# Opening the first dense unit ahead, a norm row earlier on ScalarE, transposes in another bank, and first loads from two queues

## The chip, the cores and the metric

The kernel runs on one core of a Trainium2 chip. A core has five engines that run side by side and meet through semaphores: TensorE (PE, matrix products into PSUM banks; its weight loads are listed apart as PEld), VectorE (DVE), ScalarE (ACT), GpSimd (POOL) and SyncE (SP). DMAs are issued here from SP's, ACT's and POOL's instruction streams. The metric is the time of one execution on the device, in microseconds; lower is better.

## The reference

One block of a streaming encoder, float32, 1024 frames of 1024 channels, 256 memory tokens. Cut to what matters here:

```python
h = _rmsnorm(x, norm_mix_g)
z = h @ w_in                          # 1024 x (7 * 512 + 8 + 512 + 3 * 1024)
(hq, hf, hi, hg, fq, fk, fv, ff, mq, gate_logits) = split(z)
y_a = _hgrn2_mixer(hq, hf, hi, hg, lower_bounds, hgrn_norm_g)
y_b = _fox_mixer(fq, fk, fv, ff, fox_f_bias, fox_q_norm_g, fox_k_norm_g)
mem_kv = _rmsnorm(mem, norm_mem_g) @ mem_kv_w
y_c = _memory_mixer(mq, mem_kv, mem_q_norm_g, mem_k_norm_g)
gates = sigmoid(gate_logits)
merged = gates[0] * (y_a @ w_br_hgrn) + gates[1] * (y_b @ w_br_fox) + gates[2] * (y_c @ w_br_mem)
x = x + merged @ w_out
x = x + _conv_glu_ffn(_rmsnorm(x, norm_ffn_g), w_up, conv_w, conv_b, w_down)
```

## The kernel before

Channels lie on the 128 partitions, time runs along a row. x comes as eight chunks `xk[k]` of 128 channels by 1024 frames. The norm's gain is multiplied in at once (`uh`, `ul`), and the factor 1/rms per frame is applied later, to the products. Every float32 product is made of three: an operand is split into a rounded high part and the rest, as `uh`/`ul` for x and `wh`/`wl` for weights, and `mm3` (lines 160 to 162) issues high by high, low by high and high by low. A split is a cast on ScalarE (line 166) and a subtraction on VectorE (line 174).

The part around the change is the first 100 us, up to the second dense unit:

1. The first loads: the constants `cv` (the gains among them), the first weights `wg` and the x chunks, in the order in which they are wanted. Twelve dull products (line 265) go ahead on TensorE.
2. Gate steps `s0` to `s7`: two gate chunks at once, step k with x chunk k, in four PSUM banks (two "lg", one "tr", one "po"). A step is 12 products; step k needs `uh[k]` and `ul[k]`, made by `x_chunk` (lines 346 and 347) in halves for k = 0 and 1.
3. The memory's keys and values: eight chunks `wkv` of weights (`kv_chunk`).
4. The cover: two gate chunks (`first_cover`, `gates_early`), whose products run while the x norm's factor is made. The norm: eight rows of squares (`x_square`), `rt` = (mean + eps) to the power -1/2 on POOL (line 179), then `spread_dma`: TensorE transposes `rt` (352), ScalarE copies the transpose into a row (353), two DMAs take it through DRAM into `rx`, on all partitions. Each finished gate product is then multiplied by `rx` on VectorE (461) and goes through tanh on ScalarE (462); until that has read its bank, the bank is taken.
5. The keys' transposes, in two groups of four (`mem_keys`, 410), each read out by ScalarE into `mkf` (412).
6. Dense units: a unit computes 256 channels by 1024 frames as a 2x2 product of blocks with seven products instead of eight, named by their right operand: B11, T1, T2, B22, T3, B21, T4. The T's are differences of blocks of x (`differences`, made once, in steps f1 to f3 and a last one); the left operands are the four weight blocks a11, a21, a22, a12 and their sums s1 = a21 + a22, s2 = s1 + a11, s4 = s2 + a12, s3 = a11 + a21, each split. Some products accumulate on others' banks; `snap` copies a bank ("fe") before. B21 needs nothing but a12 and x, and stands second in the first unit, sixth in the others.

What sets the order: the code issues steps in the order of the string SEQ. A planner with its own model of time then orders the instructions within each engine's stream, under the constraints of the data and of `issue_after` (an instruction that must not be placed before a given one). PSUM banks of a tag rotate.

Of the kernel before, what the change touches and what calls it, by code (L numbers as in the profile page):

```python
# [8 lines left out]
F32 = mybir.dt.float32  # L9
# [5 lines left out]
P = 128  # L15
# [76 lines left out]
def run_all(gen):  # L92
    for _ in gen:
        pass
# [15 lines left out]
def tile_block(ctx: ExitStack, tc: tile.TileContext, xT, memT, x_rows, mem_rows, vec, fbias, mats, hmask, w_first, w_cm, w_hi, w_fqk, w_fv,  # L110
# [20 lines left out]
    def ps_tr():  # L131
        return pz.tile([P, HB], F32, tag="tr", name="tr", bufs=2)
# [217 lines left out]
    def spread_dma(r, rcol, row, name, ps):  # L350

        PE.transpose(ps[:8, :P], rcol, ident)
        S.copy(row, ps[:8, :P])
# [50 lines left out]
    def mem_keys():  # L404
        mkt = keys[0]
        for hh in range(2):
            ptr = ps_tr()
            for h in range(2):
                for m in range(2):
                    PE.transpose(ptr[:, (2 * h + m) * P:(2 * h + m + 1) * P],  # L410
                                 mkt[:, m, (2 * hh + h) * P:(2 * hh + h + 1) * P], ident)
            S.activation(mkf[:, 2 * hh:2 * hh + 2, :], ptr.rearrange("p (h m) -> p h m", h=2), AF.Copy, scale=mgk)
        G.dma_start(kvd[:, 0, :], mkf.rearrange("p a b -> p (a b)"))
# [87 lines left out]
    def family_block(name, k, src, sub=None):  # L501
        h, l = fam[name]
        return split(S, h[k], l[k], src, sub)

    def differences():
# [21 lines left out]
        for k, (t2, b12, b21, b22) in enumerate(b):  # L527
            with tc.issue_after(late["x mean"].ins):
                V.scalar_tensor_tensor(out=b12, in0=b12, scalar=ngx[:, k:k + 1], in1=b22, op0=ALU.mult, op1=ALU.add)
            family_block("T3", k, b12)  # L530
        yield
        yield
        for k, (t2, b12, b21, b22) in enumerate(b):
# [5 lines left out]
            family_block("T4", k, t4[k])  # L539
        yield  # L540

    gen = {}

    def families_step():
        if "differences" not in gen:
            gen["differences"] = differences()
        next(gen["differences"])

    named = dict(f1=families_step, f2=families_step, f3=families_step, mn=mem_norm, me=keys_out, mk=mem_keys, mv=mem_values, xn=x_norm, lk=load_late, lx=lambda: load_rows(*T2[2:], *T1[2:]), ly=lambda: load_rows(*T2[:2]), lz=lambda: load_rows(*T2[2:]), ev=first_gates, cv=first_cover)
    for what in SEQ:  # L550
        if what in named:
            named[what]()
        else:
            steps[what[0]](int(what[1]))
    p0.release()

    ps1 = Rounded(tc, name="ps1", bufs=1, side="right", reuse_waits="tile")
    def block(b, k):
        if b in fam:
            return [t[k] for t in fam[b]]  # L560
# [10 lines left out]
    class Dense:  # L571
# [1 line left out]
        half = None  # L573

        def snap(self, ps):
            e = ps1.tile([P, HB], F32, tag="fe", name="fe", bufs=3)
# [6 lines left out]
        def sum_of(self, i, a, b):  # L583
            t = ps1.tile([P, HB], F32, tag=f"s{i}", name=f"s{i}")
            V.tensor_add(t, a, b)
            return t

        def operand(self, src):
# [6 lines left out]
            split(S, h, l, src)  # L595
            return h, l

    dense = Dense()

    def dense_unit(src, put, first, families):  # L600

        raw = []
        whole = None if first else dense.raw()
        for i in range(2):
            if first:
                t = wp.tile([P, 4 * 264], F32, tag="raw", name="raw", bufs=2)[:, :2 * HB]
                t = t.rearrange("p (a b) -> p a b", a=2)
            else:
                t = whole[:, 2 * i:2 * i + 2, :]
            G.dma_start(t, src[:, 2 * i:2 * i + 2, :])  # L610
            raw += [t[:, 0, :], t[:, 1, :]]
        a11, a21, a22, a12 = raw
        x, y = ps_proj(), ps_lg()
        o1 = dense.operand(a11)
        if first:
            o6 = dense.operand(a12)
        s1 = dense.sum_of(1, a21, a22)
        o2 = dense.operand(s1)
        s2 = dense.sum_of(2, s1, a11)
# [1181 lines left out]
```

## Time and profile before

| | |
|---|---|
| time, median of 3 runs | 1702.75 us (1702.54 to 1703.31) |
| the profiled execution's own time | 1703.12 us |
| its span, first to last instruction | 1701.3 us |
| TensorE busy | 1692.3 us, 99% |
| VectorE, ScalarE, GpSimd busy | 1151.9, 801.5, 326.7 us |
| granted TensorE clock | 1.00 throughout |

In rows of the profile, the first number is a start in us, the second a duration, then come engine, line of the kernel, operation, output and inputs, their shapes, and a count; what stands in square brackets is how long the engine had been idle before and what it had waited for. A product's duration is longer than its distance from the next one, as products overlap.

### The profile page before, as it was taken

Reading aid. Unit: us, or ns where it says so; the run is one execution under the profiler, and the core shown is the slowest. Engines: PE = TensorE matmul, PEld = TensorE weight load, DVE = VectorE, ACT = ScalarE, POOL = GpSimd, SP = SyncE. Lnnn points to the kernel's source line nnn. Section 1 sums busy time; section 2 is a strip of 40 time slices with the busy share of each in tenths; the row PEclk is TensorE's granted clock in tenths of the full one; section 3 lists DMA queues with packets and bytes.
Section 4 is the critical chain, followed back from the end, with each engine's and each line's share of the span. In section 5 each row is a group of like instructions: output and inputs, shape, how many; then the busy total and the mean of one; then the engine's idle time right before and its main releaser. Section 6 shows DMA issues by size and latency. Waiting matters only on the chain.

```text
span 1701.3 us, 24306 instructions
## 1 busy us (share of the span) xinstructions
PE 1692.3 (99%) x8965; PEld 1452.3 (85%) x8965; DVE 1151.9 (68%) x2057; ACT 801.5 (47%) x1428; POOL 326.7 (19%) x420
## 2 busy tenths in 40 slices
PE   9999999999999999999999999999999999999999
PEld 7788899989898998888888888888888888888887
DVE  6956555665666655786856855987778888775664
ACT  6734455555464553776531334644434444433432
POOL 0200022543433331553310000311111111100000
PEclk9999999999999999999999999999999999999999
DMA  9433242221312111200346552566555444494782
GB/s 369 170 137 114 73 146 76 77 92 45 99 50 87 52 57 57 67 27 18 100 125 216 165 188 99 162 171 172 151 144 141 118 144 147 162 375 142 247 274 87
DMA packets 82774, 227.16 MB, mean 134 GB/s; under 512 B 9680, under 2 KB 12248, under 8 KB 82528
## 3 DMA queue, kind: packets, MB, share of 16 engines
q1 hardware_dynamic: 64464, 160.99, 27.4%
q0 software_dynamic: 18048, 64.50, 13.5%
q8 instruction: 70, 1.15, 0.3%
q14 instruction: 48, 0.39, 0.1%
q10 hardware_dynamic: 144, 0.13, 0.0%
HBM read 180.72 MB, written 67.93 MB: 146 GB/s over the span
## 4 chain that ended last, share of the span: by engine, by line
PE 98%; DVE 1%; DMA 0%; ACT 0%; issue 0%; SPq 0%; DVEq 0%
PE pp L162 21%; PE pp L160 21%; PE pp L161 21%; PE lg L160 4%; PE lg L162 4%; PE lg L161 4%; PE tr L160 3%; PE tr L162 3%; PE tr L161 3%; PE po L951 1%; PE lg L910 1%; PE lg L909 1%; PE po L950 1%; PE po L160 1%; PE po L161 1%; PE po L162 1%
## 5 line engine op out<-in xcount | busy, mean ns | idle before, releaser
L160 PE MATMUL pp<-uh,wh 128*128 128x512 f32 x412 | 163.1, 396 | 0.0
L161 PE MATMUL pp<-ul,wh 128*128 128x512 f32 x412 | 162.9, 395 | 0.0
L162 PE MATMUL pp<-uh,wl 128*128 128x512 f32 x412 | 162.4, 394 | 0.0
L161 PE MATMUL pp<-wl,uh 128*128 128x256 f32 (+1 forms) x512 | 146.2, 286 | 0.0
L162 PE MATMUL pp<-wh,ul 128*128 128x256 f32 (+1 forms) x512 | 146.0, 286 | 0.0
L160 PE MATMUL pp<-wh,uh 128*128 128x256 f32 (+1 forms) x512 | 145.6, 285 | 0.0
L166 ACT CAST wh<-s 128x512 fp32r<-128x512 f32 x113 | 68.2, 620 | 130.8 <-PE pp L161 66.4
L166 ACT CAST wh<-raw 128x1024 fp32r<-128x1024 f32 (+2 forms) x76 | 67.7, 890 | 100.3 <-PE pp L161 88.2
L166 ACT CAST wh<-rw 128x512 fp32r<-128x512 f32 x87 | 53.2, 619 | 107.6 <-PE pp L161 72.0
L160 PEld LDWEIGHTS pp<-wh,uh 128*128 128x128 f32 x512 | 97.3, 190 | 1.2
L161 PEld LDWEIGHTS pp<-wl,uh 128*128 128x128 f32 x512 | 97.4, 190 | 1.0
L162 PEld LDWEIGHTS pp<-wh,ul 128*128 128x128 f32 x512 | 97.4, 190 | 0.9
L1443 POOL DMA_DIRECT2D rw<-in_w_up x44 | 24.1, 555 | 372.8 <-DVE wl L1336 171.8
L166 ACT CAST dwh<-wr 128x1024 fp32r<-128x1024 f32 (+1 forms) x41 | 40.2, 980 | 115.0 <-PE tr L161 40.4
L162 PEld LDWEIGHTS pp<-uh,wl 128*128 128x128 f32 x412 | 77.5, 188 | 15.1
L174 DVE TENSOR_TENSOR wl<-raw,wh 128x1024 fp32r<-128x1024 f32 (+2 forms) x75 | 78.0, 1040 | 18.1 <-ACT wh L166 17.9
L160 PEld LDWEIGHTS pp<-uh,wh 128*128 128x128 f32 x412 | 77.5, 188 | 14.6
L161 PEld LDWEIGHTS pp<-ul,wh 128*128 128x128 f32 x412 | 77.5, 188 | 14.5
L174 DVE TENSOR_TENSOR dwl<-wr,dwh 128x1024 fp32r<-128x1024 f32 (+1 forms) x41 | 46.3, 1130 | 33.6 <-ACT dwh L166 32.5
L925 ACT ACTIVATE pt<-pt,st 128x128 f32<-128x128 f32 (+3 forms) x64 | 49.7, 777 | 40.1 <-DVE st L922 32.0
L927 POOL TENSOR_SCALAR pt<-pt,st 128x128 f32<-128x128 f32 (+3 forms) x64 | 50.7, 793 | 77.5 <-DVE st L926 62.4
L1336 DVE TENSOR_TENSOR wl<-rw,wh 128x512 fp32r<-128x512 f32 x69 | 47.7, 705 | 22.5 <-PE pp L162 18.1
(497 smaller groups left out, 5123.9 us busy)
## 6 DMA issues: line engine op xcount, KB each, us to landing
rw<-in_w_up POOLq DMA_DIRECT2D x44, 512.0 KB, 4.9
sd<-in_w_dn POOLq DMA_DIRECT2D x30, 512.0 KB, 6.2
br<-yd SPq DMA_DIRECT2D x30, 512.0 KB, 5.3
raw<-in_w_cm SPq DMA_DIRECT2D x24, 512.0 KB, 3.4
gd<-gt SPq DMA_DIRECT2D x48, 256.0 KB, 2.0
gt<-gd SPq DMA_DIRECT2D x48, 256.0 KB, 2.7
yd<-fc SPq DMA_DIRECT2D x44, 256.0 KB, 3.0
wr<-sd SPq DMA_DIRECT2D x20, 512.0 KB, 4.6
```

The lines of the kernel that those rows point to most:

```text
L160: PE.matmul(ps, lh, rh, start=first, stop=False, skip_group_check=more)
L161: PE.matmul(ps, lh, rl, start=False, stop=False, skip_group_check=more)
L162: return PE.matmul(ps, ll, rh, start=False, stop=last, skip_group_check=more)
L166: return S.copy(out, in_)
L174: return (sub or V).tensor_sub(l, src, h.bitcast(F32))
L909: PE.matmul(ps[:, :w], qa[i][:, tsl], kh[i][:, s0:s0 + w], start=True, stop=False)
L910: fox_sets[p][3] = PE.matmul(ps[:, :w], qa[i][:, tsl], kl[i][:, s0:s0 + w], start=False, stop=True)
L925: S.activation(pt[:, :ns], pt[:, :ns], AF.Exp, bias=st[:, 2:3], accum_out=st[:, 3:4])
L927: G.tensor_scalar(pt[:, :ns], pt[:, :ns], st[:, 3:4], 0.0, ALU.mult, ALU.add)
L950: PE.matmul(o, vhl[:, sb, :], ph[:, src], start=(sb == 0), stop=False)
L1336: late["split"] = V.tensor_sub(l, src, h.bitcast(F32))
L1443: late["raw"] = G.dma_start(raw[:, 2 * i:2 * i + 2, :], src[:, 2 * i:2 * i + 2, :])
```

## The change

- First loads. ACT's queue takes the first quarter of the first weights, then `cv`, then the second quarter and the remaining half; SP's queue takes x chunks 0 and 1 in halves, then the other chunks as before. Before, ACT issued only the first quarter, and SP `cv`, chunk 0 in halves, the other three quarters in one piece and chunk 1 whole.
- Eight dull products instead of twelve.
- The row's copy is remembered (`late["row"]`), and T1's casts, T3's casts and the first unit's opening are issued after it.
- The keys' transposes are made in the bank of the second group of values, `pkv[1][1]`, and no longer take two from the rotation of "tr".
- `Dense.open` makes a unit's loads and its operands up to s2. For the first unit it is called as step `du` of SEQ, behind f3 and ahead of `ev` and `mk`, with the sums in places of x chunks that are no longer read; it also splits a12 and s2 there, and the unit splits s4 before T4 is made.
- The small constants of the recurrence are issued after the cover's split instead of at the end of the program's first part.

```diff
-NDULL = 12
+NDULL = 8
...
-       "q0 me k4 q1 k5 c0 ly c1 lz q2 q3 k6 q4 q5 k7 d0 q6 q7 xn d1 mv f1 cv f2 ev mk f3").split()
+       "q0 me k4 q1 k5 c0 ly c1 lz q2 q3 k6 q4 q5 k7 d0 q6 q7 xn d1 mv cv f1 f2 f3 du ev mk").split()
...
-    SP.dma_start(cv, vec)
     S.dma_start(wg[0][:, :256], w_first[0][:, :256])
-    for i in range(2):
-        SP.dma_start(xk[0][:, i * HB:(i + 1) * HB], xT[:, 0, i * HB:(i + 1) * HB])
-    SP.dma_start(wg[0][:, 256:], w_first[0][:, 256:])
-    for k in range(1, KC):
+    S.dma_start(cv, vec)
+    for k in range(2):
+        for i in range(2):
+            sl = slice(i * HB, (i + 1) * HB)
+            SP.dma_start(xk[k][:, sl], xT[:, k, sl])
+        sl = slice(256 + 256 * k, 512 + 512 * k)
+        S.dma_start(wg[0][:, sl], w_first[0][:, sl])
+    for k in range(2, KC):
...
-        S.copy(row, ps[:8, :P])
+        late["row"] = S.copy(row, ps[:8, :P])
...
-            ptr = ps_tr()
+            ptr = pkv[1][1]
...
-            with tc.issue_after(late["square"].ins):
+            with tc.issue_after(late["row"].ins):
                 S.activation(h, b11, AF.Copy, scale=col(C_GX + k))
...
-            family_block("T3", k, b12)
+            with tc.issue_after(late["row"].ins):
+                family_block("T3", k, b12)
...
+        def open(self, src, places=None):
+            raw = []
+            whole = None if places else self.raw()
+            for i in range(2):
...
+                G.dma_start(t, src[:, 2 * i:2 * i + 2, :])
+                raw += [t[:, 0, :], t[:, 1, :]]
+            a11, a21, a22, a12 = raw
+            o1 = self.operand(a11)
+            o6 = self.operand(a12) if places else None
+            s1 = self.sum_of(1, a21, a22, places and places[0])
+            o2 = self.operand(s1)
+            s2 = self.sum_of(2, s1, a11, places and places[1])
+            return raw, o1, o6, o2, s2, self.operand(s2) if places else None
...
+    def first_unit():
+        with tc.issue_after(late["row"].ins):
+            gen["unit"] = dense.open(w_pair[0], (xk[4][:, HB:], xk[5][:, HB:]))
...
+        raw, o1, o6, o2, s2, o3 = gen["unit"] if first else dense.open(src)
...
-        product(x, dense.operand(s2), "T2", False)
+        product(x, o3 or dense.operand(s2), "T2", False)
         e2 = dense.snap(x)
+        o4 = dense.operand(dense.sum_of(4, s2, a12, xk[6][:, HB:] if first else None))
         run_all(families)
-        s4 = dense.sum_of(4, s2, a12)
-        product(y, dense.operand(s4), "B22", False)
+        product(y, o4, "B22", False)
...
+    with tc.issue_after(late["keys"].ins), tc.issue_after(late["x_low"].ins):
+        small_consts()
     families = gen["differences"]
...
-    small_consts()
```

What the planner makes of it. First the issues of SP's and ACT's queues at the start; `xk_102` to `xk_104` are x chunks 0 to 2, `wg_155` and `wg_147` the first weights, `wg_156` and `wg_148` the next. SP before:

```order
L273 DMA cv<-in_vec 128x125
L276 DMA xk_102<-in_xT 128x512 x2
L277 DMA wg_155<-in_w_first 128x768
L281 DMA xk_103<-in_xT 128x1024
L281 DMA xk_104<-in_xT 128x1024
L280 DMA wg_156<-in_w_first 128x1024
L281 DMA xk_105<-in_xT 128x1024
```

and now:

```order
L278 DMA xk_102<-in_xT 128x512 x2
L278 DMA xk_103<-in_xT 128x512 x2
L284 DMA xk_104<-in_xT 128x1024
L283 DMA wg_148<-in_w_first 128x1024
L284 DMA xk_105<-in_xT 128x1024
```

ACT before:

```order
L274 DMA wg_155<-in_w_first 128x256
L299 ACT_TABLE_LOAD
L299 ACTIVATE warm<-mhalf 128x1
L166 CAST wh<-wg_155 128x256
L317 ACTIVATE lbe_3128<-lbe_3128 128x4
```

and now:

```order
L273 DMA wg_147<-in_w_first 128x256
L274 DMA cv<-in_vec 128x125
L280 DMA wg_147<-in_w_first 128x256
L280 DMA wg_147<-in_w_first 128x512
L302 ACT_TABLE_LOAD
L302 ACTIVATE warm<-mhalf 128x1
L166 CAST wh<-wg_147 128x256
```

`cv` and two pieces of the weights have gone from SP to ACT, ahead of the table load, and chunk 1 comes in halves directly behind chunk 0.

TensorE around the keys' second group of transposes (`ident,mkt`): what follows them, before (`uh_79` is the high part of x chunk 0, `uh_87` of chunk 4):

```order
L162 MATMUL pp<-uh_93,wl 128x512
L410 MATMUL tr<-ident,mkt 128x128 x4
L160 MATMUL tr<-uh_87,wh 128x512
L161 MATMUL tr<-ul_88,wh 128x512
L162 MATMUL tr<-uh_87,wl 128x512
L160 MATMUL tr<-uh_89,wh 128x512
```

and now:

```order
L162 MATMUL pp<-uh_93,wl 128x512
L413 MATMUL tr<-ident,mkt 128x128 x4
L160 MATMUL pp<-uh_79,wh 128x512
L161 MATMUL pp<-ul_80,wh 128x512
L162 MATMUL pp<-uh_79,wl 128x512
L160 MATMUL pp<-uh_81,wh 128x512
```

The twelve products of B21 (into "tr") have moved; now they stand between B11 and T1:

```order
L161 MATMUL pp<-ul_86,wh 128x512
L162 MATMUL pp<-uh_85,wl 128x512
L160 MATMUL tr<-uh_87,wh 128x512
L161 MATMUL tr<-ul_88,wh 128x512
L162 MATMUL tr<-uh_87,wl 128x512
L160 MATMUL tr<-uh_89,wh 128x512
...
L161 MATMUL tr<-ul_94,wh 128x512
L162 MATMUL tr<-uh_93,wl 128x512
L160 MATMUL lg<-T1h_607,wh 128x512
L161 MATMUL lg<-T1l_609,wh 128x512
```

In place of them the cover's second half (into "pp") follows the transposes.

ScalarE from the last read of the values (`mkt`) on; `line` is the norm's row, `raw` the first unit's weights, `s_775` and `s_781` its sums s1 and s2. Before:

```order
L386 ACTIVATE mkt<-tr,rm 128x512
L517 ACTIVATE T1h_548<-xk_102,cv 128x512
L517 ACTIVATE T1h_548<-xk_103,cv 128x512
L517 ACTIVATE T1h_549<-xk_104,cv 128x512
L517 ACTIVATE T1h_549<-xk_105,cv 128x512
L166 CAST wh<-raw 128x512
L166 CAST T3h_678<-xk_102 128x512
L166 CAST T3h_678<-xk_103 128x512
L166 CAST wh<-raw 128x512
L353 COPY line<-pp 8x128
L166 CAST T3h_678<-xk_104 128x512
```

and now:

```order
L389 ACTIVATE mkt<-tr,rm 128x512
L356 COPY line<-pp 8x128
L520 ACTIVATE T1h_607<-xk_102,cv 128x512
L520 ACTIVATE T1h_607<-xk_103,cv 128x512
L520 ACTIVATE T1h_608<-xk_104,cv 128x512
L520 ACTIVATE T1h_608<-xk_105,cv 128x512
L166 CAST T3h_643<-xk_102 128x512
L166 CAST T3h_643<-xk_103 128x512
L166 CAST T3h_643<-xk_104 128x512
L166 CAST wh<-raw 128x512 x2
L166 CAST T3h_643<-xk_105 128x512
L166 CAST T2h_627<-xk_102 128x512
```

The row's copy has gone ahead of T1's four casts, and both casts of raw weights stand together. Further on the sums were cast behind (s1) and among T4's casts; before:

```order
L412 ACTIVATE mkf<-tr,mgk 128x512
L462 ACTIVATE gt<-gt 128x512 x7
L166 CAST wh<-s_775 128x512
L577 COPY fe<-pp 128x512
L166 CAST T4h_851<-t4s_701 128x512
L166 CAST T4h_851<-t4s_702 128x512
L166 CAST T4h_851<-t4ta 128x512
L166 CAST T4h_851<-t4tb 128x512
L462 ACTIVATE gt<-gt 128x512
L166 CAST wh<-s_781 128x512
L166 CAST wh<-s_882 128x512
L577 COPY fe<-lg 128x512
```

and now, where `xk_106`, `xk_107` and `xk_108` hold s1, s2 and s4 in their second halves:

```order
L465 ACTIVATE gt<-gt 128x512 x2
L166 CAST wh<-xk_107 128x512
L465 ACTIVATE gt<-gt 128x512
L166 CAST wh<-xk_108 128x512
L565 COPY fe<-pp 128x512
L465 ACTIVATE gt<-gt 128x512
L166 CAST wh<-raw 128x512
L465 ACTIVATE gt<-gt 128x512
L565 COPY fe<-lg 128x512
L166 CAST T4h_860<-t4s_711 128x512
L166 CAST T4h_860<-t4s_712 128x512
L166 CAST T4h_860<-t4ta 128x512
```

The casts of s2 and s4 now stand ahead of T4's, and that of s1 some rows further up; T4's run behind the copies of the banks of B11 ("fe<-pp") and T1 ("fe<-lg").

More of the change, by code (lines that the diff above doesn't have):

```diff
@@ L540, in differences @@
         yield
[L542 to L557, printed above, removed]
     def block(b, k):
@@ L575, in snap @@
         def snap(self, ps):
-            e = ps1.tile([P, HB], F32, tag="fe", name="fe", bufs=3)
+            e = home["sums"].tile([P, HB], F32, tag="fe", name="fe", bufs=3)
             S.copy(e, ps)
@@ L581, in raw, with sum_of @@
             return home["raw"].tile([P, 4, HB], F32, tag="rw", name="rw", bufs=2)
-        def sum_of(self, i, a, b):
-            t = ps1.tile([P, HB], F32, tag=f"s{i}", name=f"s{i}")
+        def sum_of(self, i, a, b, t=None):
+            t = t if t is not None else home["sums"].tile([P, HB], F32, tag=f"s{i}", name=f"s{i}")
             V.tensor_add(t, a, b)
@@ L596, in operand @@
             return h, l
-    dense = Dense()
-    def dense_unit(src, put, first, families):
[L602 to L611, printed above, removed]
+        def open(self, src, places=None):
+            raw = []
+            whole = None if places else self.raw()
+            for i in range(2):
+                if places:
+                    t = wp.tile([P, 4 * 264], F32, tag="raw", name="raw", bufs=2)[:, :2 * HB]
+                    t = t.rearrange("p (a b) -> p a b", a=2)
+                else:
+                    t = whole[:, 2 * i:2 * i + 2, :]
+                G.dma_start(t, src[:, 2 * i:2 * i + 2, :])
[7 more added lines that the diff above has]
+            return raw, o1, o6, o2, s2, self.operand(s2) if places else None
@@ new lines, in tile_block, with families_step @@
+    dense = Dense()
+    gen = {}
+    def families_step():
+        if "differences" not in gen:
+            gen["differences"] = differences()
+        next(gen["differences"])
+    def first_unit():
+        with tc.issue_after(late["row"].ins):
+            gen["unit"] = dense.open(w_pair[0], (xk[4][:, HB:], xk[5][:, HB:]))
+    named = dict(du=first_unit, f1=families_step, f2=families_step, f3=families_step, mn=mem_norm, me=keys_out, mk=mem_keys, mv=mem_values, xn=x_norm, lk=load_late, lx=lambda: load_rows(*T2[2:], *T1[2:]), ly=lambda: load_rows(*T2[:2]), lz=lambda: load_rows(*T2[2:]), ev=first_gates, cv=first_cover)
@@ L612, in dense_unit @@
+    for what in SEQ:
+        if what in named:
+            named[what]()
+        else:
+            steps[what[0]](int(what[1]))
+    p0.release()
+    ps1 = home["sums"] = Rounded(tc, name="ps1", bufs=1, side="right", reuse_waits="tile")
+    def dense_unit(src, put, first, families):
+        raw, o1, o6, o2, s2, o3 = gen["unit"] if first else dense.open(src)
         a11, a21, a22, a12 = raw
         x, y = ps_proj(), ps_lg()
-        o1 = dense.operand(a11)
-        if first:
-            o6 = dense.operand(a12)
@@ L617, in dense_unit @@
-        s1 = dense.sum_of(1, a21, a22)
-        o2 = dense.operand(s1)
-        s2 = dense.sum_of(2, s1, a11)
         product(x, o1, "B11", True)
```

## The prediction

> **What bounds the kernel now.** I read the page's first part, then TensorE's waits over the whole span, then the timeline of the first 92 us. The page:
>
> ```profile
> span 1701.3 us, 24306 instructions
> PE 1692.3 (99%) x8965; PEld 1452.3 (85%) x8965; DVE 1151.9 (68%) x2057; ACT 801.5 (47%) x1428; POOL 326.7 (19%) x420
> ```
>
> TensorE is busy in all but 9.0 us of the span, so a change that leaves the products alone can win only where TensorE stands still. The waits of TensorE (longest first: total, times, longest):
>
> ```profile
> PE pp L160 <- ACT wh L166: 1.1, 1, 1.1
> ...
> PE lg L160 <- ACT uh L346: 1.0, 3, 0.5
> PE tr L160 <- ACT mkf L412: 0.8, 1, 0.8
> PE po L1175 <- DVE St L1181: 0.7, 1, 0.7
> PE pp L162 <- DVE wl L174: 0.5, 1, 0.5
> ```
>
> (The row left out is the first instruction's start.) All but the L1175 row fall into the first 92 us, where the diff works. So there are two places: the first loads (L346) and the first dense unit (L166, L174, L412).
>
> **The first dense unit and the transposes.** TensorE's timeline there:
>
> ```profile
> 62.37 0.60 PE L410 MATMUL tr<-ident,mkt 128*128 128x128 f32 x4
> 62.73 0.48 PE L160 MATMUL pp<-uh,wh 128*128 128x512 f32 x1
> 63.04 0.40 PE L161 MATMUL pp<-ul,wh 128*128 128x512 f32 x1
> ...
> 68.30 0.60 PE L410 MATMUL tr<-ident,mkt 128*128 128x128 f32 x4
> 69.67 0.50 PE L160 MATMUL tr<-uh,wh 128*128 128x512 f32 x1 [0.78 <-ACT mkf L412]
> ...
> 83.01 0.39 PE L161 MATMUL lg<-T1l,wh 128*128 128x512 f32 x1
> 83.24 0.39 PE L162 MATMUL lg<-T1h,wl 128*128 128x512 f32 x1
> 84.68 0.50 PE L160 MATMUL pp<-T2h,wh 128*128 128x512 f32 x1 [1.05 <-ACT wh L166]
> 85.02 0.40 PE L161 MATMUL pp<-T2l,wh 128*128 128x512 f32 x1
> 85.90 0.50 PE L162 MATMUL pp<-T2h,wl 128*128 128x512 f32 x1 [0.48 <-DVE wl L174]
> ```
>
> A product starts 0.23 us after the one before (83.01 to 83.24); by starts, the losses are larger than the waits' own figures. After the second transposes 69.67 - 68.30 = 1.37, where the first took 62.73 - 62.37 = 0.36: 1.01 lost. Then 1.44 - 0.23 = 1.21, and 0.88 - 0.23 = 0.65. A start after a wait costs 0.34 instead of 0.23 to the next one; three such, of which the one after the second transposes stays (63.04 - 62.73 = 0.31): 0.22. Together 3.1 us.
>
> Why they are there: the unit's B21 product stood behind the second transposes in the same bank, so it waited for ScalarE to read that bank (L412). T2's operand is the sum s2, whose cast stood behind four T4 casts:
>
> ```profile
> 68.93 0.69 ACT L412 ACTIVATE mkf<-tr,mgk 128x512 f32<-128x512 f32 x1 [3.55 <-PE tr L410]
> ...
> 81.41 1.14 ACT L166 CAST T4h<-t4s 128x512 fp32r<-128x512 f32 x2
> ...
> 84.02 0.61 ACT L166 CAST wh<-s 128x512 fp32r<-128x512 f32 x1
> ```
>
> ```profile
> 67.65 1.28 DVE L461 TENSOR_TENSOR gt<-pp,rx 128x512 f32<-128x512 f32 x2
> 68.85 0.68 DVE L461 TENSOR_TENSOR gt<-lg,rx 128x512 f32<-128x512 f32 x1
> ```
>
> In the new order B21 comes after B11, in the other tr bank, and the casts and sums of s1, s2, s4 stand ahead of T4. Do they arrive in time? I step the new order on the old clock, with 0.53 us for a cast on ScalarE (1.14 for two less 0.61 for one) and 0.60 for an operation on VectorE (67.65 to 68.85 for two). The norm's row starts it:
>
> ```profile
> 54.36 2.09 POOL L179 TENSOR_TENSOR rt<-rt,mhalf 128x8 f32<-128x8 f32 x1 [0.64 <-DVE rt L178]
> 55.60 0.68 ACT L386 ACTIVATE mkt<-tr,rm 128x512 f32<-128x512 f32 x1
> 56.77 0.27 PE L352 MATMUL pp<-ident,rt 128*8 128x128 f32 x1
> 60.70 0.25 ACT L353 COPY line<-pp 8x128 f32<-8x128 f32 x1
> ```
>
> The copy moves from 60.70 to the end of the row's transpose, 57.05: 3.65 us earlier. Since it stands directly behind mkt, done at 56.28, ScalarE now idles 0.8 us, with T1, T3 and the raw casts queued behind it; T1 starts at 57.3, 1.1 later. For T1's casts VectorE waits, until 58.0, and TensorE only at the unit. rx, the row's way through DRAM, was there at 67.65 at the latest (VectorE had not idled), so now by 64.0. VectorE has eleven operations from 58.0 to the first gate: 65, not 67.65.
>
> TensorE: 23 products from 63.04 to 68.30 make 0.228 each, 24 are 5.5 and a unit's twelve 2.74. Its steps, against the last of what each wants, counted in the new rows:
>
> - cover's second half 68.7, against 65.8 (the gate has read its bank);
> - B11 74.2, against 67.0 (low part, three operations into the gates);
> - B21 76.9, against 70.1 (low part, five rows on);
> - T1 79.7, against 73.1 (s1's low part, five more);
> - T2 82.4, against 77.6 (B11 has ended at 76.9 and is copied);
> - B22 85.1, against 83.1 (T1 has ended at 82.4 and is copied);
> - T3 87.9, against 86.4: T4's four casts to 85.2, the copy of T2 to 85.8, s3's cast; its low part at 87.0, wanted 0.45 after T3's start.
>
> So all 3.1 us go, and s3, with 1.4 us, is late next. Ends: 0, if a wait of like size opens at T3 or at the next unit, and 3.2, with slower starts behind the waits; I take 3.1, as every step has room.
>
> **The first loads.** TensorE, ScalarE and VectorE at the start, and what the DMA moved (rows by stretch, GB/s last; then packets per queue between 2 and 3 us, q10 being ScalarE's):
>
> ```profile
> 5.09 0.69 PE L160 MATMUL lg<-uh,wh 128*128 128x512 f32 x1 [0.27 <-ACT uh L346]
> ...
> 10.25 0.50 PE L160 MATMUL lg<-uh,wh 128*128 128x512 f32 x1 [0.51 <-ACT uh L346]
> ...
> 10.87 0.50 PE L160 MATMUL lg<-uh,wh 128*128 128x512 f32 x1
> ```
>
> ```profile
> 3.21 0.17 DVE L326 TENSOR_SCALAR ngx<-cv 128x4 f32<-128x4 f32 x1 [3.21 <-DMA cv<-in_vec]
> 4.32 0.72 ACT L346 ACTIVATE uh<-xk,cv 128x512 fp32r<-128x512 f32 x1
> 9.48 2.41 ACT L346 ACTIVATE uh<-xk,cv 128x512 fp32r<-128x512 f32 x3 [0.54 <-DMA xk<-in_xT]
> ```
>
> ```profile
> 1.00:3.60 2.60, 2.57 (x12) 2.57 (x13) 0.39 (x5) 1.67 (x3) 0.00 (x0) 1.00 0.64 180
> 1.00:7.60 6.60, 6.04 (x27) 5.39 (x28) 3.23 (x16) 3.63 (x7) 0.00 (x0) 1.00 0.82 248
> ```
>
> ```profile
> q1 hardware_dynamic: 132, 0.11, 46.4%
> q10 hardware_dynamic: 140, 0.13, 37.5%
> ```
>
> With products back to back from its 10.87 start the second step would have begun at 10.4. After: the rows give 0.47 MB moved by 3.6 and 1.64 MB by 7.6 us, 0.29 MB/us. The two queues took turns packet by packet (132 to 140), so I pair the pieces: first weights with x's first half, 0.39 MB at 3.3 us; cv with the second half, 0.72 MB at 4.5; second weights with the first half of x chunk 1, 1.11 MB at 5.8; the last weights with its second half, 1.64 MB at 7.6. Landing lags the bytes: 0.46 MB moved at 3.6 was used at 4.32, 1.64 MB moved at 7.6 at 9.48. So 0.7 growing to 1.9: landings about 4.0, 5.5, 7.2, 9.5. cv, which scales every x chunk, lands 2.3 us later than before and starts the first product at 6.25 instead of 5.09. But then nothing is missing: the second half of x is scaled at 6.9, ten more products end at 9.2. The second step starts there, its third product wants the last half of chunk 1, 9.5 + 0.72 = 10.2, against 10.87: 0.6 us won. Ends: -1.2 (no wait after the first product) and +0.5 (the last piece a microsecond later than I think).
>
> [...]
>
> Can TensorE use 0.6 us here? The memory's first weights are the next thing that it meets:
>
> ```profile
> 27.04 2.36 DVE L174 TENSOR_TENSOR wl<-wkv,wh 128x1024 fp32r<-128x1024 f32 x2 [0.69 <-ACT wh L166]
> 30.03 0.39 PE L161 MATMUL pp<-wl,umh 128*128 128x512 f32 x1
> ```
>
> The first of these two ends by 28.3, wanted at 30.03: 1.7 us to spare. At the row's transpose (56.77, its input ready at 56.45) 0.3 us is to spare, and two Exps and two small VectorE operations now stand in that chain. ngx's row, 0.17 for 128x4, prices one: 0.34 on the engine that ends last, so 0.0 to 0.4 of wait, and I put 0.1, since part of each overlaps the next. The other small constants, at 0.17 each some 1.5 us of VectorE, move from the first loads, where VectorE waits, to the next 50 us, where it has gaps: nothing. The four dull products removed stood in TensorE's waits: nothing. ScalarE issues three more DMAs ahead of its table load, all before cv lands. On POOL's queue no row changes place; on SP's, one raw cover load and one wkv swap, and one gate's store and one mqd store, none of which anyone waits for in the rows above. The planner also swaps a few rows near 1090 us; the list of waits has nothing from there among its longest: nothing, give or take 0.3.
>
> **Sum.** 3.1 + 0.6 - 0.1 = 3.6 us off the span of 1701.3. The profiled run took 1703.12, 1.8 more than its span and 0.37 above the median; I take the 3.6 from the median: 1699.15, some 0.21% less. What a measurement here can tell from no change is about 0.2%, 3.4 us: the forecast lies on that edge.
>
> **Rivals.**
> - The start gives nothing or loses 0.5: cv is late for certain, and the last pieces land where xk landed before. 1702.75 - 3.0 or - 2.5: 1699.7 to 1700.2. Chance 0.2. [...]
> - The wait moves to T3: s3's cast stands behind T4's casts, which wait for the copy of T1. It decides from 1.4 us late; at 3 us late, 1.6 come back: 1701. For: seven rows ahead of s3 on ScalarE wait for TensorE or for T4. Against: 1.4 us to spare. Chance 0.17.
> - The planner's order doesn't do it: B21, only moved, meets its wait elsewhere and the middle wins nothing: 1702. Chance 0.06.
> - Slower: TensorE's clock. Eight dull products end at 4.8, and now nothing follows until 6.25.
>
> ```profile
> 1.03 3.78 PE L265 MATMUL tr<-dull,mhalf 128*128 128x128 f32 x16 [1.03 <-POOL dull L263]
> 5.62 0.60 PE L265 MATMUL tr<-dull,mhalf 128*128 128x128 f32 x4
> ```
>
> The first sixteen start 0.22 us apart, the four at 5.62 about 0.1, and the product at 5.09 takes 0.69 where that at 10.25 takes 0.50: the array got faster at some 5 us. If the gap undoes this, products go at 0.45 for a while, 0.2 each; from the 19th on the gain of 3.6 is eaten, and three steps of twelve would cost 7.2: 1706. [...] Chance 0.05, and a part of it inside 0.2%.
>
> The forecast's own chance is 0.52 (1698.2 to 1700.2 on its own). Faster by over 0.2% is below 1699.35: 0.45 from the forecast's half and better starts, 0.04 from the first rival. Slower: 0.04 from the clock. The range leaves out the clock and the planner's case: 1697.6 (start -1.2, middle 3.2, with 0.8 for other rows) to 1701.7.
>
> **What would show it.** Right: no wait on mkf and none on L166 or L174 between 60 and 100 us; the row's copy at 57; the first product after 5.5, the second step before 9.7, its third product near 10.2. Wrong: cv landing by 4 us, a wait at T3 (near 87), a new wait at the first wkv product or at the row's transpose, products 0.4 apart before 12 us.

## The result, and the profile after

The changed kernel takes 1700.07 us (median; 1698.40 to 1701.36), the kernel before, timed beside it, 1702.85 us (1702.40 to 1704.71): a ratio of 0.998, 95% interval 0.9973 to 0.9986. That is 2.8 us or 0.16% less, inside the predicted range and 0.9 us slower than the predicted 1699.2. The profiled execution took 1700.23 us with a span of 1698.4, 2.9 less than the span before.

The times of the changed kernel fall into two groups: seven of the 22 lie between 1698.40 and 1698.65, fourteen between 1699.2 and 1700.4, one at 1701.36. The profiled execution belongs to the upper group. Why there are two turned out to be the main question.

TensorE's waits over the span, all of them:

```profile
PE lg L160 <- ACT uh L349: 1.8, 1, 1.8
PE tr L265 <- POOL dull L263: 1.0, 1, 1.0
PE po L1189 <- DVE St L1195: 0.7, 1, 0.7
PE pp L162 <- DVE wl L1350: 0.2, 1, 0.2
```

The waits on L166, L174 and `mkf`, at the first dense unit and the transposes, are gone, and nothing has taken their place. TensorE's timeline there (the second transposes, and the first products of the cover's second half, B11, B21, T1, T2, B22 and T3; the last row is T3's first product with the low part of s3):

```profile
68.68 0.60 PE L413 MATMUL tr<-ident,mkt 128*128 128x128 f32 x4
69.03 0.48 PE L160 MATMUL pp<-uh,wh 128*128 128x512 f32 x1
...
74.60 0.39 PE L160 MATMUL pp<-uh,wh 128*128 128x512 f32 x1
...
77.32 0.39 PE L160 MATMUL tr<-uh,wh 128*128 128x512 f32 x1
...
80.04 0.39 PE L160 MATMUL lg<-T1h,wh 128*128 128x512 f32 x1
...
82.76 0.39 PE L160 MATMUL pp<-T2h,wh 128*128 128x512 f32 x1
...
85.48 0.39 PE L160 MATMUL lg<-uh,wh 128*128 128x512 f32 x1
...
88.20 0.39 PE L160 MATMUL pp<-T3h,wh 128*128 128x512 f32 x1
...
89.10 0.39 PE L162 MATMUL pp<-T3h,wl 128*128 128x512 f32 x1
```

From B11 on each stage lasts 2.72 us, back to back. ScalarE and VectorE in the same place:

```profile
57.49 0.26 ACT L356 COPY line<-pp 8x128 f32<-8x128 f32 x1 [0.67 <-PE pp L355]
...
82.96 0.59 ACT L565 COPY fe<-lg 128x512 f32<-128x512 f32 x1 [1.79 <-PE lg L162]
83.44 1.14 ACT L166 CAST T4h<-t4s 128x512 fp32r<-128x512 f32 x2
...
86.16 0.62 ACT L166 CAST wh<-s 128x512 fp32r<-128x512 f32 x1
```

```profile
65.46 1.27 DVE L464 TENSOR_TENSOR gt<-pp,rx 128x512 f32<-128x512 f32 x2
...
87.11 0.68 DVE L174 TENSOR_TENSOR wl<-s,wh 128x512 fp32r<-128x512 f32 x1
```

The start went otherwise. TensorE there, with the cover's first product and the row's transpose as the last rows:

```profile
1.03 3.48 PE L265 MATMUL tr<-dull,mhalf 128*128 128x128 f32 x16 [1.03 <-POOL dull L263]
6.30 0.50 PE L160 MATMUL lg<-uh,wh 128*128 128x512 f32 x1 [1.79 <-ACT uh L349]
6.64 0.40 PE L160 MATMUL tr<-uh,wh 128*128 128x512 f32 x1
6.92 0.50 PE L160 MATMUL lg<-uh,wh 128*128 128x512 f32 x1
7.25 0.57 PE L160 MATMUL po<-uh,wh 128*128 128x512 f32 x1
7.62 0.63 PE L161 MATMUL lg<-ul,wh 128*128 128x512 f32 x1
8.04 0.63 PE L162 MATMUL lg<-uh,wl 128*128 128x512 f32 x1
...
10.60 0.45 PE L162 MATMUL po<-uh,wl 128*128 128x512 f32 x1
10.90 0.39 PE L160 MATMUL lg<-uh,wh 128*128 128x512 f32 x1
...
51.74 0.39 PE L160 MATMUL pp<-uh,wh 128*128 128x512 f32 x1
...
57.18 0.27 PE L355 MATMUL pp<-ident,rt 128*8 128x128 f32 x1
```

VectorE's first use of `cv`, and the scaling of the last half of x chunk 1 on ScalarE:

```profile
5.46 0.17 DVE L329 TENSOR_SCALAR ngx<-cv 128x4 f32<-128x4 f32 x1 [5.46 <-DMA cv<-in_vec]
...
7.68 0.72 ACT L349 ACTIVATE uh<-xk,cv 128x512 fp32r<-128x512 f32 x1
```

The first product starts at 6.30, but behind the fourth the products stand 0.43 us apart instead of 0.23, until 10.6. No wait is named in these rows: the products themselves are slow. The granted clock by stretch (it is the last figure but two) shows it, where the page's forty slices, 42 us each, do not:

```profile
6.00:7.20 1.20, 0.90 (x3) 0.58 (x4) 1.12 (x3) 1.20 (x3) 0.00 (x0) 1.00 1.03 401
7.20:8.00 0.80, 0.80 (x3) 0.61 (x3) 0.80 (x2) 0.80 (x3) 0.00 (x0) 0.57 1.12 410
8.00:9.00 1.00, 1.00 (x4) 0.76 (x3) 1.00 (x3) 1.00 (x3) 0.00 (x0) 0.50 0.96 369
...
10.00:10.60 0.60, 0.60 (x2) 0.41 (x2) 0.03 (x1) 0.15 (x1) 0.00 (x0) 0.50 1.03 403
10.60:12.00 1.40, 1.40 (x7) 1.18 (x6) 0.37 (x1) 1.27 (x2) 0.00 (x0) 0.95 1.01 410
```

It is 0.50 from about 7.3 to 10.7 us. In the kernel before it was 1.00 throughout the first 12 us.

**Where the 2.9 us are.** From its start at 51.74 on, the cover follows without a wait until the unit, so one can split the span there. Before, the cover's first product started at 51.33:

```profile
51.33 0.39 PE L160 MATMUL pp<-uh,wh 128*128 128x512 f32 x1
```

Behind it came 1701.3 - 51.33 = 1650.0 us, now 1698.4 - 51.74 = 1646.7. So the middle won 3.3 us, and the start lost 0.4 in the profiled executions (0.7 by the medians of the changed kernel and of the middle alone). The same two numbers, for every kernel that follows:

| kernel | median, us | cover starts | the rest |
|---|---|---|---|
| before | 1702.85 | 51.33 | 1650.0 |
| changed | 1700.07 | 51.74 | 1646.7 |
| middle alone | 1699.38 | 50.82 | 1646.8 |
| loads alone | 1703.55 | 52.08 | 1649.9 |
| twelve dull products | 1698.76 | 50.66 | 1646.6 |
| cv first | 1698.78 | 50.05 | 1646.7 |
| four dull products | 1700.41 | 52.11 | 1646.7 |
| bank alone | 1702.90 | 50.93 | 1650.0 |
| row late | 1699.61 | 49.95 | 1647.8 |
| row late, bank back | 1699.65 | 50.17 | 1647.7 |
| row alone | 1701.53 | 50.84 | 1648.4 |
| before, twenty dull products | 1705.99 | 52.85 | 1651.2 |
| cv on SP | 1698.59 | 50.36 | 1646.7 |
| cv on SP, sixteen dull products | 1699.79 | 50.74 | 1647.3 |

Medians are of 7 to 22 executions; the two last columns are of one profiled execution each. The rest agrees within 0.2 us wherever the order of the middle is the same. The cover's start varies with the landing of the first loads: 50.82 to 51.33 for the four profiled kernels that have the old start unchanged. The kernel before, timed beside each group, had medians of 1702.85, 1703.08, 1703.43 and 1703.27; ratios below are to the one timed beside it.

### The profile page after: what moved, and what is told of

It is laid out like the page before. It is cut to its first block, busy times and chain, and to the rows that moved or that the text cites. A ratio compares the mean times of both kernels' runs of the same rounds, so it can differ in the third digit from the quotient of the medians.

```text
span 1698.4 us, 24291 instructions
## 1 busy us (share of the span) xinstructions
PE 1691.0 (100%) x8957; PEld 1452.4 (86%) x8957; DVE 1150.8 (68%) x2057; ACT 800.9 (47%) x1428; POOL 324.6 (19%) x420
## 4 chain that ended last, share of the span: by engine, by line
PE 99%; DVE 0%; ACT 0%; DMA 0%; issue 0%; ACTq 0%; DVEq 0%
PE pp L160 21%; PE pp L162 21%; PE pp L161 21%; PE lg L160 4%; PE lg L162 4%; PE lg L161 4%; PE tr L162 3%; PE tr L161 3%; PE tr L160 3%; PE po L966 1%; PE lg L925 1%; PE lg L924 1%; PE po L965 1%; PE po L160 1%; PE po L161 1%; PE po L162 1%
## 5 line engine op out<-in xcount | busy, mean ns | idle before, releaser
L166 ACT CAST wh<-s 128x512 fp32r<-128x512 f32 x110 | 66.5, 621 | 131.6 <-PE pp L161 55.1
L166 ACT CAST wh<-raw 128x1024 fp32r<-128x1024 f32 (+2 forms) x76 | 67.6, 890 | 100.6 <-PE pp L161 86.2
L166 ACT CAST wh<-rw 128x512 fp32r<-128x512 f32 x87 | 53.2, 619 | 108.1 <-PE pp L161 70.2
L166 ACT CAST dwh<-wr 128x1024 fp32r<-128x1024 f32 (+1 forms) x41 | 40.2, 980 | 115.8 <-PE tr L161 40.0
L174 DVE TENSOR_TENSOR wl<-raw,wh 128x1024 fp32r<-128x1024 f32 (+2 forms) x75 | 78.0, 1040 | 17.8 <-ACT wh L166 17.6
L174 DVE TENSOR_TENSOR dwl<-wr,dwh 128x1024 fp32r<-128x1024 f32 (+1 forms) x41 | 46.3, 1129 | 31.7 <-ACT dwh L166 31.7
```

Source lines behind the costliest of these rows:

```text
L166: return S.copy(out, in_)
L174: return (sub or V).tensor_sub(l, src, h.bitcast(F32))
```

## The experiments

**Middle alone and loads alone.** The changed kernel with the old first loads and twelve dull products:

```diff
-NDULL = 8
+NDULL = 12
...
+    SP.dma_start(cv, vec)
     S.dma_start(wg[0][:, :256], w_first[0][:, :256])
-    S.dma_start(cv, vec)
-    for k in range(2):
-        for i in range(2):
-            sl = slice(i * HB, (i + 1) * HB)
-            SP.dma_start(xk[k][:, sl], xT[:, k, sl])
-        sl = slice(256 + 256 * k, 512 + 512 * k)
-        S.dma_start(wg[0][:, sl], w_first[0][:, sl])
-    for k in range(2, KC):
+    for i in range(2):
+        SP.dma_start(xk[0][:, i * HB:(i + 1) * HB], xT[:, 0, i * HB:(i + 1) * HB])
+    SP.dma_start(wg[0][:, 256:], w_first[0][:, 256:])
+    for k in range(1, KC):
```

and the kernel before with the new first loads and eight dull products, the same edit the other way round.

> The changed kernel with the first loads and the twelve dull products of the kernel before; so the middle part of the change alone (order of the first dense unit, the norm's row, the keys' transposes, the small constants). Theory: the middle is worth 3.2 us by itself (3.3 less 0.1), so 1702.8 - 3.2 = 1699.6, with the row's transpose at 56.8 as before, and no second group of times 1.7 us apart from the first, since the dull products are spread to 8 us and TensorE's rate does not fall. Rival, the middle's gain hangs on the start (its casts come in time only as the start is late): 1700.5 or more, with a wait on a cast between 60 and 100 us.

> The kernel before with nothing but the new first loads and eight dull products. Theory (the first step's products run at half rate in most executions because TensorE has stood still for 1.8 us): times in two groups, 1702.8 + 0.4 = 1703.2 in most executions and 1703.2 - 1.7 = 1701.5 in the others; profile with some nine products 0.43 us apart after 7 us, or none if it is one of the others. Rival, half rate is a matter of chance in any start: the kernel before would show the two groups as often as this one. Rival of the prediction, the start wins 0.6: all at 1702.2.

Middle alone: 1699.38 (1698.85 to 1700.06, nine runs), ratio 0.9977 (0.9968 to 0.9987), the rest 1646.8, no wait between 60 and 100 us. The middle's gain does not hang on the start. Loads alone: 1703.55 (1702.21 to 1706.5, eleven runs), ratio 1.0000 (0.9992 to 1.0009), the rest as before. Its cover starts at 52.08, and its granted clock is 0.50 in the same place:

```profile
8.00:9.00 1.00, 1.00 (x3) 0.78 (x3) 1.00 (x4) 1.00 (x4) 0.00 (x0) 0.50 0.94 295
```

So the whole gain comes from the middle, and the new start, as it is, gives nothing. By the medians it loses 0.5 to 0.7 (1703.55 against 1703.08, 1700.07 against 1699.38), a loss that the interval does not tell from none. The lower group foreseen for it, at 1701.5, was not clearly there: one run of eleven is at 1702.21, the next at 1703.32. Why it is rarer here than the seven of 22 in the changed kernel is not shown.

**The gap ahead of the first product.** Four dull products fewer, four more, and four more with cv ahead of the first weights:

```diff
-NDULL = 8
+NDULL = 4
```

```diff
-NDULL = 8
+NDULL = 12
```

```diff
-NDULL = 8
+NDULL = 12
...
-    S.dma_start(wg[0][:, :256], w_first[0][:, :256])
     S.dma_start(cv, vec)
+    S.dma_start(wg[0][:, :256], w_first[0][:, :256])
```

> The changed kernel with twelve dull products in place of eight, all twelve ahead of the first product; so TensorE stands still from some 5.6 to 6.3 us instead of 4.5 to 6.3. Theory (idle gap): the half rate goes, the upper group of times at 1700.2 with it, and the median is 1698.5 or a little less. [...]

> The changed kernel with cv ahead of the first quarter of the weights in ScalarE's queue, and twelve dull products ahead of the first product. cv should land 0.5 to 1.0 us earlier than 5.46, the first product start at 5.4 to 5.8, and the dull products fill nearly the whole time ahead of it. Theory (idle gap): no half rate, and the start is then bound by the loads, not by cv: 1698.0 to 1698.5. Rival, the loads bound the start, and half rate comes by chance: two groups as in the changed kernel, median 1700.1.

> The changed kernel with four dull products in place of eight: TensorE stands still from 2.8 to 6.3 us. Theory (idle time ahead of the first product sets the rate): half rate from the first product on, for 13 to 17 products of 0.2 more each, 2.6 to 3.4 against 1.8, and in every execution, so 1698.6 + 2.6 to 3.4 = 1701.2 to 1702.0 without a group at 1698.5. Rival (chance): the same two groups as the changed kernel, 1698.5 and 1700.1.

Twelve: 1698.76 (1698.61 to 1699.19, eight runs), ratio 0.9973 (0.9962 to 0.9983). The upper group is gone, which would have stayed if the gap had no part in it. The start of its timeline, and of that with four:

```profile
1.03 4.87 PE L265 MATMUL tr<-dull,mhalf 128*128 128x128 f32 x24 [1.03 <-POOL dull L263]
6.84 0.50 PE L160 MATMUL lg<-uh,wh 128*128 128x512 f32 x1 [0.94 <-ACT uh L349]
...
8.02 0.40 PE L161 MATMUL lg<-ul,wh 128*128 128x512 f32 x1
8.26 0.39 PE L162 MATMUL lg<-uh,wl 128*128 128x512 f32 x1
```

```profile
1.03 2.08 PE L265 MATMUL tr<-dull,mhalf 128*128 128x128 f32 x8 [1.03 <-POOL dull L263]
6.36 0.79 PE L160 MATMUL lg<-uh,wh 128*128 128x512 f32 x1 [3.25 <-ACT uh L349]
6.95 0.63 PE L160 MATMUL tr<-uh,wh 128*128 128x512 f32 x1
7.38 0.63 PE L160 MATMUL lg<-uh,wh 128*128 128x512 f32 x1
...
10.79 0.41 PE L161 MATMUL po<-ul,wh 128*128 128x512 f32 x1
```

With twelve, TensorE stands still for 0.94 us, the granted clock is 1.00 throughout the first 12 us and the products go 0.23 apart from the fourth on, though here the first one started 0.5 later than in the changed kernel (the profiled execution is the slowest of the eight). With four it stands still for 3.25 us, and the products are 0.43 apart from the second, at 6.95, to 10.4; the time is 1700.41 (1699.76 to 1700.99, eleven runs) and the lower group is gone instead. It was 0.8 less than the least I had expected: the slow stretch held ten products, not 13 to 17. cv first: 1698.78 (1698.49 to 1698.99, seven runs), ratio 0.9973 (0.9963 to 0.9984), no half rate (clock 1.00 in the first 12 us, products 0.23 apart from the fourth on). Its cv landed at 4.0 instead of 5.5, but the first product still started at 6.23, since now the first weights came late: their cast stands at 5.15 instead of 4.61. With twelve dull products and the old order it stood at 5.19 in the profiled execution, so one profile of each does not tell the order's part from the execution's.

In these profiles, then, the half rate goes with the gap: at 1.79 and 1.94 us the clock fell to 0.50, at 0.94 us or none it stayed at 1.00. As lengthening the dull products also gives TensorE more to do just before, no run tells the length of the gap from the share of some longer stretch in which TensorE was busy. The number of dull products ahead is not it, since middle alone has the same eight there, a gap of 0.29 us, and a clock of 1.00. The two groups, some 1.7 us apart, I take to be the same program with and without the slow stretch. That the lower group of the changed kernel lacks the stretch is inferred: its times are those of the kernel with twelve, but none of its executions was profiled; nor is it shown why one execution has the stretch and another has not.

**The parts of the middle.** The kernel before with only the keys' transposes in the values' bank; then the changed kernel with twelve dull products and the row late again, and that with the old banks as well:

```diff
-            ptr = ps_tr()
+            ptr = pkv[1][1]
```

```diff
-            with tc.issue_after(late["row"].ins):
+            with tc.issue_after(late["square"].ins):
                 S.activation(h, b11, AF.Copy, scale=col(C_GX + k))
...
-            with tc.issue_after(late["row"].ins):
-                family_block("T3", k, b12)
+            family_block("T3", k, b12)
```

```diff
-            ptr = pkv[1][1]
+            ptr = ps_tr()
```

> The kernel before with nothing but the keys' transposes in the values' bank; B21 keeps its place behind the second transposes, and T2's cast its place behind T4's. Theory (the three waits add up, since ScalarE's chain to T2's cast starts from B11's bank and moves with TensorE): the 1.0 behind the transposes goes, the waits at T2 of 1.2 and 0.65 stay, 1702.8 - 1.0 = 1701.8. Rival (T2's cast stands on the norm's row, which does not move): what is won behind the transposes comes back at T2, 1702.6 to 1702.8 with a wait of 2.2 on L166.

> The changed kernel with twelve dull products, in which T1's and T3's casts need not wait for the norm's row any more: the row's copy stands behind T1's casts again, and B21 moves back to directly behind the second transposes, which use the values' bank. Theory (the row only decides when the gates' banks come free, and B21's 2.7 us cover for that): no new wait, 1698.8 as with the row early. Rival (the row early is what makes the middle's gain): rx is there some 3 us later, the cover's second half or T3 waits, 1 to 3 us, 1699.8 to 1701.8.

> As row_late, and the keys' transposes take two banks from the rotation of tr again, as in the kernel before. Theory: B21 behind the transposes waits for ScalarE's read of that bank again, 1.0 more than row_late, 1699.8, with a wait named mkf near 68 us; T2's waits do not come back, since s2's cast stays ahead of T4's. Rival (the bank is not what B21 waited for): as row_late.

Bank alone: 1702.90 (1702.11 to 1704.58, eleven runs), ratio 0.9997 (0.9988 to 1.0006). Neither expectation held: the time is within 0.1 of the rival's, but its reason is not there, for the wait on `mkf` is simply still there, and T2's waits are as they were:

```profile
69.27 0.51 PE L160 MATMUL tr<-uh,wh 128*128 128x512 f32 x1 [0.78 <-ACT mkf L412]
...
84.28 0.50 PE L160 MATMUL pp<-T2h,wh 128*128 128x512 f32 x1 [1.05 <-ACT wh L166]
```

"tr" rotates over two banks, and the edit takes two fewer from it: B21 lands in the bank of the last transposes either way. The other two kernels confirm that the bank does nothing: 1699.61 (1699.46 to 1699.99, ten runs) and 1699.65 (1699.47 to 1699.93, eleven). Both have B21 behind the transposes and the same wait:

```profile
66.94 0.60 PE L413 MATMUL tr<-ident,mkt 128*128 128x128 f32 x4
68.31 0.51 PE L160 MATMUL tr<-uh,wh 128*128 128x512 f32 x1 [0.78 <-ACT mkf L415]
```

Their rest is 1647.7 to 1647.8, 1.1 more than with the row early and 2.2 less than before, without any wait at T2. So the row late costs 1.1 (0.9 by the medians), where the theory had 0, but by B21's place alone; the late rx, which the rival of that run had in mind, delays nothing, as no other wait is listed. And the bank put back costs nothing, where the theory had 1.0.

**The row alone.** The kernel before with the row first on ScalarE (the first pair of lines is the end of the string SEQ):

```diff
-mv f1 cv f2 ev mk f3
+mv cv f1 f2 f3 ev mk
...
-        S.copy(row, ps[:8, :P])
+        late["row"] = S.copy(row, ps[:8, :P])
...
-            with tc.issue_after(late["square"].ins):
+            with tc.issue_after(late["row"].ins):
...
+            with tc.issue_after(late["row"].ins):
+                family_block("T3", k, b12)
```

> The kernel before with the norm's row first on ScalarE (T1's and T3's casts behind it, and the differences' steps behind the cover's first step so that they can be); no opening ahead, no other bank, old loads. B21 then stands between B11 and T1, and s2's cast still behind T4's four. Theory A (the parts add: the row moves B21 and wins its 1.0, the early opening wins T2's 1.9 to 2.2): 1702.8 - 1.0 = 1701.8 with a wait on L166 near 82 us. Theory B (B21's 2.7 us between B11 and T1 also cover T2's casts, so that either part alone removes T2's waits): s2's cast at 80 to 81 us against a T2 wanted at 82, 1702.8 - 3.2 = 1699.6 and no wait on L166 between 60 and 100 us.

1701.53 (1701.03 to 1701.80, eleven runs), ratio 0.9987 (0.9978 to 0.9995); the rest 1648.4, so 1.6 won: between the two theories, nearer to A. TensorE, ScalarE and VectorE at T2:

```profile
82.02 0.39 PE L160 MATMUL pp<-T2h,wh 128*128 128x512 f32 x1
82.24 0.39 PE L161 MATMUL pp<-T2l,wh 128*128 128x512 f32 x1
83.82 0.50 PE L162 MATMUL pp<-T2h,wl 128*128 128x512 f32 x1 [1.19 <-DVE wl L174]
```

```profile
80.82 0.61 ACT L166 CAST wh<-s 128x512 fp32r<-128x512 f32 x1
```

```profile
80.07 1.28 DVE L174 TENSOR_TENSOR T4l<-t4s,T4h 128x512 fp32r<-128x512 f32 x2
...
81.88 0.69 DVE L174 TENSOR_TENSOR T4l<-t4tb,T4h 128x512 fp32r<-128x512 f32 x1
82.48 0.68 DVE L586 TENSOR_TENSOR s<-raw 128x512 f32<-128x512 f32 x1
83.08 0.68 DVE L174 TENSOR_TENSOR wl<-s,wh 128x512 fp32r<-128x512 f32 x1
```

As theory B had it, B21 between B11 and T1 gives s2's cast its time: done at 81.4, wanted at 82.0. But the subtraction behind that cast stands on VectorE behind four T4 subtractions and a sum, and ends at 83.8. The row alone wins 1.6, the opening without the early row 2.2 (row late), both 3.3: they overlap by 0.5.

**Other starts.** cv first on SP's queue, with twelve and with sixteen dull products:

```diff
+    SP.dma_start(cv, vec)
     S.dma_start(wg[0][:, :256], w_first[0][:, :256])
-    S.dma_start(cv, vec)
```

> The changed kernel with cv first on SP's queue, ahead of x, and the weights' pieces alone on ScalarE's; twelve dull products, ten of them ahead of the first product. cv lands near 3.3 us as in the kernel before. Theory (with the rate kept, the start is set by the last of the first 1.6 MB): first product at 5.1 to 5.4, and the second step no earlier than 9.2 to 9.7, so 1698.0 to 1698.7, no better than cv_first by more than 0.5. Rival (cv's landing sets the start): 0.9 less than cv_first, 1697.9.

> As cv_on_sp with sixteen dull products, the four more between the products of the first and second gate step. Theory (rate): if cv_on_sp shows a second group of times, this one does not; else the four cost 0.1 each at most: within 0.4 of cv_on_sp. Rival (dull products only take time): 0.4 more than cv_on_sp in every execution.

1698.59 (1698.37 to 1699.42, seven runs), ratio 0.9972 (0.9961 to 0.9983), and 1699.79 (1699.17 to 1700.31, eleven runs). cv landed at 3.4, but x only for a scaling at 5.38; the first product started at 6.15 and the second step at 9.56. Like cv first, this gives nothing beyond shortening the gap, to 1.07 us here. Sixteen cost 1.2 by the medians, which neither expectation had. In the profiled executions the rest is 0.5 longer, in the planner's new order (with a new wait of 0.3 at 228.94, for L781), and the cover starts 0.4 later, the rival's figure; but there the loads had come earlier, with the first product at 5.58, so that the four dull products cost more than that at the start.

The best versions are the three with the gap at 1.07 us or less, 1698.6 to 1698.8, some 4.3 to 4.7 us (0.27%) under the kernel before and 1.3 to 1.5 under the median of the changed one.

**The kernel before's own late runs.** Of the 29 to 32 runs of the kernel before timed beside the last groups, 11 to 16 lie above 1703.5. Twenty dull products in place of twelve:

```diff
-NDULL = 12
+NDULL = 20
```

> The kernel before with twenty dull products in place of twelve; the eight more stand in the first three gate steps, between products that wait for loads. The kernel before shows times in two groups, most near 1702.7 and some from 1703.6 to 1705. Theory (the upper group is TensorE's rate falling after the waits of the first steps): the upper group goes, median 1702.5 to 1703.0 since a dull product costs up to 0.1 where nothing is waited for. Rival (the upper group comes from loads that land later, or from the middle): both groups stay.

1705.99 (1705.42 to 1706.51, eleven runs), ratio 1.0014 (1.0005 to 1.0023). There is one group, but at a higher time than either: the cover starts at 52.85, and the planner's order has a new wait in T1:

```profile
84.27 0.50 PE L162 MATMUL lg<-T1h,wl 128*128 128x512 f32 x1 [1.41 <-DVE wl L174]
```

With two things changed it decides nothing. Middle alone and row alone have the old loads and no run of 20 in a second group of that kind, bank alone has three of eleven, which points to the middle with the row late rather than to the start; no profile fell on such a run, and the cause stays open.

## Why the prediction was right, and where it was not

- **The middle, 3.1 us.** Right: 3.3. The stages came at 74.60 to 88.20, predicted 74.2 to 87.9, with the 0.3 to 0.4 of the start on top. The first gate read its bank at 65.46 (65 predicted), and s3, named as late next with 1.4 us, had its low part done at 87.79 for a product at 89.10: 1.3. Of the reason given for the 1.0 behind the transposes, "the other tr bank" is wrong: the bank changes nothing, and the place behind B11 does it, which the planner gives B21 when the row comes early.
- **The wait of 0.1 at the row's transpose.** Not there: the transpose starts 5.44 us behind the cover's start, as before (57.18 - 51.74, and 56.77 - 51.33).
- **The start, 0.6 won.** The step that failed is "ten more products end at 9.2". cv landed at 5.46 (5.5 predicted) and the first product started at 6.30 (6.25), and the last half of chunk 1 was scaled from 7.68, earlier than the predicted 9.5. But the products went at half rate (0.43 us apart, clock 0.50), the sign "products 0.4 apart before 12 us" that the prediction had named against itself: the first step ended at 10.9, 1.7 late, and what was to be a gain of 0.6 became a loss of 0.4 in the profiled execution (the cover at 51.74 against 51.33). Where the gap is short the size of the term was right: the changed loads with twelve dull products have a median 0.6 below the old loads with the same middle (1698.76 and 1699.38). That is in part luck. The prediction had the second step wait for the last half of chunk 1, and no product of that step waited in any profiled execution with the new loads; and single profiles put the cover anywhere from 0.2 to 1.4 us earlier than with the old loads (49.95 to 50.66 with twelve dull products, against 50.82 to 51.33). Chunk 1's two halves had been issued by 2.54 us in the changed kernel, where its issue began at 2.59 in the kernel before. No run separates the order, the pieces and the two queues.
- **The clock rival.** Its price was right, 0.2 for each product, and so was its place; it held for eight products and not for the 19 from which it would have eaten the gain. A chance of 0.05 was far too small: by their times it came in some 15 of 22 executions. The range left this case out, and the time stayed inside it since the slow stretch held eight products; twice as many, at 0.2 each, would have put it at the upper bound of 1701.7. That the range held is luck to that extent. The chance was my estimate and rested on no row: TensorE's longest wait behind its first product before, 1.05 us at T2, was followed by a clock of 1.00, and nothing told what a gap of 1.5 us would do. Here 1.79 us without a product were followed by 3.4 us at a clock of 0.50, with 0.43 us between starts for 512 columns.
- **The rival that the start gives nothing,** at 1699.7 to 1700.2, names the time that came, for another reason than cv and the last pieces: cv landed when the forecast had it, and the last half of chunk 1 earlier.
- **"The four dull products removed stood in TensorE's waits: nothing."** Wrong, and the same step: they cost nothing while they ran, and their cover was the rate of what came next. Put back, and all ahead of the first product, they are worth 1.3 us by the medians.

## What to carry over

Dull products ahead of the first real ones are to be sized by when the first operands land, not by count: behind a gap of 1.79 us the clock fell to 0.50 here, behind one of 0.94 us it did not. When a change makes the first product later, lengthen them by as much, and look at the distance of the products behind the gap, since no wait showed what was lost there. When a product is moved out of a wait, ask whether its place or its buffer does it; of a rotation of two, taking two fewer changed nothing here. Parts that seem to add (1.6 and 2.2 here) may cover the same wait, so take each away alone before pricing them.

## What the runs showed of the hardware

TensorE's granted clock in the records of the changed kernel fell to 0.50 for about 3.4 us after a gap of 1.79 us, and not at once: three products behind the gap, from 6.30 to 7.25, still went at 0.28 to 0.34 us, as the first three do with twelve dull products at a clock of 1.00. The fall came 2.8 us after the last dull product. Behind the 1.94 us of loads alone it was much the same: four products 0.23 to 0.34 us apart, then a clock of 0.50. Behind the gap of 0.94 us (twelve dull products) the clock stayed at 1.00, and behind that of 1.07 us (cv on SP) the products went 0.23 us apart from 7.27 on. With four dull products ahead the products were 0.43 us apart from 6.95 to 10.37, yet the records give the clock as 1.00 there:

```profile
9.00:10.00 1.00, 1.00 (x4) 0.72 (x3) 0.83 (x2) 1.00 (x4) 0.00 (x0) 1.00 1.01 397
```

So the column shows the fall of the clock to 0.50, but not the slow products of this start. Nor does it move in the kernel before, where the dull products were 0.22 us apart up to 4.8 us and about 0.1 at 5.62. The distance of the products shows both.
